# A third gate projection ahead of the last SSD output projection, memory norms inside the SSD, and a convolution that goes on below later projections

## The chip, the cores and the metric

The kernel runs on one core of a Trainium2 chip. The metric is device time in microseconds (us) of one execution. Five engines work in parallel, each through its own rows in order: TensorE (PE in the profile, with its weight loads as PEld), VectorE (DVE), ScalarE (ACT), GpSimd (POOL) and SyncE (SP, which here only starts DMAs; ACT and POOL start some too). An engine waits for another by semaphores.

## What is computed

One layer of a streaming encoder with 512 prompt tokens, 64 sample tokens and 256 memory rows. The normed input goes through one large projection, three branches are computed from it and merged by sigmoid gates:

```python
h = _rmsnorm(x, norm_pre_w); proj = h @ w_in     # split: glu_v, glu_g, conv_gate, z, xbc, dt, q, xa_gate, gates
u = glu_v * jax.nn.sigmoid(glu_g)
c, new_a = _causal_dwconv(u, st_a, conv_dw_w, conv_dw_b)         # width 31
c = jax.nn.silu(_layernorm(c, conv_ln_w, conv_ln_b)) * jax.nn.silu(conv_gate)
out_a = c @ conv_out_w
y, new_h = _ssd_scan(xh, dt, a, B, C, st_h)                      # 4 groups of 8 heads
yg = (y + xh * ssd_d) * silu(z)                                  # per group:
yg = yg * lax.rsqrt(jnp.mean(yg * yg, axis=-1, keepdims=True) + EPS)
out_b = (yg * ssd_norm_w) @ ssd_out_w
k, v = split(_rmsnorm(mem, mem_norm_w) @ xa_kv_w)                # prompt memory; the sample uses a cache
p = jax.nn.softmax(einsum(q, k) * 256 ** -0.5); o = einsum(p, v)  # 4 heads
out_c = (o * jax.nn.silu(xa_gate)) @ xa_out_w
m = g[0] * out_a + g[1] * out_b + g[2] * out_c                   # g = sigmoid(gates + gate_b)
x_new = x + _rmsnorm(m @ w_out, norm_post_w)
```

All data are float32. Matmuls run on operands that are split into a high and a low part, with three products (high·high, high·low, low·high), so a projection of 128 output channels over 576 tokens and 1024 inputs is 2 × 8 × 3 = 48 matmuls.

## The kernel before

Channels lie on partitions and the T = 576 tokens along the free axis. The program is one stream of stages; in the profiled execution they lie as follows.

- **SSD, 0 to 440 us**: four groups of heads. For group g, `gating_a` (from L627) makes the sum of squares, `gating_b` (from L644) the norm: two ones-matmuls (L649, L650) sum over partitions, ACT takes the root (L652), DVE the reciprocal (L653) and the product (L657), and a high/low split follows (L616, L618). `out_b` then projects the group; its four weight tiles are named ob0_0 to ob3_3. The output projections of groups 0 to 2 are fill work of the next group's scan.
- **End of the SSD, 440 to 500 us**: `glu(0)`, `gating_b(3)`, `glu(1)`, the combinations T1 to T4 of the input for the next stage, `out_b(3, ...)`, `glu(2)`. A `glu(j)` is two projections, gg (its tanh on ACT) and gv (the product on DVE), and puts the result into the convolution's buffer `u`; POOL copies its tails (L736 to L740).
- **Pairs, 500 to 720 us**: 17 pairs of projections in a scheme of seven products P1 to P7 (`slot`, L905). DVE and ACT form the sums of weights (L875 to L888) and combine the products. Gated results go out through rows of the buffer `ob` to DRAM (msc, L944). At product P5 of pair 8, `mem_prep` loads the 256 memory rows into rows of `ob` that a store has freed (L1004) and norms them: Square and Sqrt on ACT (L270, L271), reciprocal and product on DVE (L272, L274).
- **Start of attention, 720 to 740 us**: q0, q1, then eight transposes of the memory to channels on partitions (`tr_act`, PE L331, ACT L333, DVE L334).
- **Attention, 740 to 890 us**: for each head, k and q of two tiles each, then the transposes of the head before (P, L1174), its output, then v, scores (L1113 to L1115) and softmax (L1098 to L1107). q0 and q1 come from the stage before; heads 1 to 3 project q between the k projections. cg0 and cg1 follow.
- **Merges, 890 to 1100 us**: `oc` (8 projections of the attention output), `cg2` to `cg7` (conv gates), `g0` (8 first merge gates), `oa` (8 projections of the convolution branch). `ln_mean` and `ln_rstd` do the layer norm over channels with ones-matmuls (L1265, L1266); between them and `oa`, channel tile by channel tile, stand the product with the norm, a tanh, the product with the gate and a split (L1300 to L1308, L620).
- **w_out and the last norm, 1100 to 1141 us.**

**The convolution** is background work: 8 channel tiles, each with a first step on ACT, 30 taps on DVE (L816, 606 columns, of which 576 count) and an `add` that sums over channels into `csum`. These steps lie in a list `bg`; `bgrun(n)` emits the next n at a place of the program, at raised priority. Places with a `bgrun`: every other product in the pair stage, the projections, scores and outputs of attention (2 to 6 each time), the oc merges (10 each); `bgrun(10000)` behind them emits the rest.

**The order on each engine** is made by a scheduler that simulates the program's dependencies; a priority moves an instruction forward. What an engine does first is therefore seen in its rows, not in the code.

**Weights**: the list `order` names each weight tile in the order of use; two tiles ahead (LA), `prep_to` loads one by SP into one of three buffers, makes the high part on ACT (L189) and the low part in one of two ways: a subtraction on DVE (L191), used up to the position `hold` (all that comes before attention) and for k and v, or a negated copy on ACT (L193) to which a DMA of POOL adds the raw weights (L194).

## Time and profile before

| what | us |
|---|---|
| median of 3 executions (1141.1 to 1145.8) | 1141.92 |
| the profiled execution itself | 1143.13 |
| its span in the profile | 1141.4 |
| mean granted clock of PE | 0.986 |

A window of the profile is read as: window, its length, then busy time and number of instructions for PE, PEld, DVE, ACT and POOL, the clock that PE was granted, the busy share of the DMA engines, GB/s. The stages of the program:

```profile
0.00:440.00 440.00, 435.46 (x3351) 415.54 (x3352) 344.73 (x598) 233.76 (x449) 41.84 (x122) 1.00 0.41 115
440.00:500.00 60.00, 47.00 (x340) 45.03 (x339) 45.70 (x63) 24.23 (x34) 13.23 (x12) 0.89 0.20 58
500.00:720.00 220.00, 211.44 (x1559) 208.83 (x1558) 165.51 (x246) 142.26 (x247) 60.30 (x65) 0.99 0.80 189
740.00:890.00 150.00, 142.11 (x1050) 135.88 (x1048) 139.65 (x214) 87.72 (x168) 9.49 (x11) 0.97 0.64 162
1100.00:1141.40 41.40, 34.48 (x152) 23.86 (x150) 17.31 (x33) 11.89 (x28) 0.00 (x0) 0.98 0.17 58
```

A busy PE is not PE at its peak: a matmul that runs at a lower clock is busy for longer. A line of the timeline gives start, duration, engine, line and operation, output and inputs, shapes, and in brackets how long the engine was idle before it and who released it.

### The profile page before, as it was taken

To read this page: it belongs to the slowest core of one execution; us is meant where nothing else is said; L and a number is where in the kernel's file an instruction comes from. 1 tells how busy PE (TensorE), PEld (TensorE's weight loads), DVE (VectorE), ACT (ScalarE), POOL (GpSimd) and SP (SyncE) were. 2 spreads that over 40 slices of the span, in tenths; PEclk is the share of its full clock that TensorE was granted. 3 is DMA by queue.
4 is the path that set the end of the run, shared out by engine and by line. 5 is a ranking of instruction groups with operands and counts; after the bars stand their busy time and mean duration, and the time that the engine had idled before them with its cause. 6 is when DMAs were issued, how large, how long until landed. Compare 5 with 4: busy or idle time off the path is not lost.

```text
span 1141.4 us, 20485 instructions
## 1 busy us (share of the span) xinstructions
PE 1097.9 (96%) x8081; PEld 1052.2 (92%) x8081; DVE 868.8 (76%) x1371; ACT 606.4 (53%) x1065; POOL 148.3 (13%) x237
## 2 busy tenths in 40 slices
PE   8999999999999999599989999899999999999997
PEld 8999999999999999599989999899898999999974
DVE  5778898488969886946787887389999998685433
ACT  5665655464537432535676666474457234685331
POOL 0100110020002100313224321000001011111000
PEclk9999999999999999799999999999999999999999
DMA  7354423442443323167887887666567786788812
GB/s 204 94 169 130 126 83 107 123 113 79 116 115 99 93 63 100 37 144 153 209 198 158 182 211 198 180 161 167 147 161 185 206 208 150 160 180 196 230 45 83
DMA packets 201495, 164.55 MB, mean 144 GB/s; under 512 B 14935, under 2 KB 175743, under 8 KB 201399
## 3 DMA queue, kind: packets, MB, share of 16 engines
q1 hardware_dynamic: 187142, 126.55, 38.8%
q0 software_dynamic: 13104, 34.35, 16.7%
...
## 4 chain that ended last, share of the span: by engine, by line
PE 84%; DVE 7%; issue 3%; DMA 3%; ACT 2%; POOL 0%; DVEq 0%; SPq 0%; ACTq 0%; POOLq 0%
PE mm L214 55%; PE X L905 7%; DVE c L816 3%; PE Y L905 3%; PE ps L214 3%; PE Z L905 2%; PE ps L1114 2%; PE ps L1115 2%; PE ps L1113 2%; DMA pl<-rawb 2%; PE ps L573 2%; PE ps L599 2%; PE ps L577 1%; DVE wlo L191 1%; PE ps L538 1%
## 5 line engine op out<-in xcount | busy, mean ns | idle before, releaser
L214 PE MATMUL mm<-hT,whi 128*128 128x288 f32 (+2 forms) x2240 | 397.3, 297 | 1.0 <-ACT ob L668 0.5
L214 PEld LDWEIGHTS mm<-hT,whi 128*128 128x128 f32 x2240 | 334.3, 189 | 3.4 <-issue 1.3
L214 PE MATMUL mm<-hT,wlo 128*128 128x288 f32 (+2 forms) x1120 | 246.4, 298 | 0.0
L189 ACT ACTIVATE whi<-raw 128x1024 fp32r<-128x1024 f32 x118 | 124.8, 1057 | 216.2 <-PE mm L214 169.1
L816 DVE SCALAR_TENSOR_TENSOR c<-u,dww,c 128x606 f32<-128x606 f32 x240 | 199.6, 846 | 2.8 <-ACT c L809 0.3
L214 PEld LDWEIGHTS mm<-hT,wlo 128*128 128x128 f32 x1120 | 184.8, 189 | 1.3 <-issue 0.7
L191 DVE TENSOR_TENSOR wlo<-raw,whi 128x1024 fp32r<-128x1024 f32 x78 | 95.2, 1221 | 51.2 <-ACT whi L189 50.8
L214 PE MATMUL mm<-hi,whi 128*128 128x288 f32 x512 | 112.3, 301 | 10.8 <-DVE xs L657 10.8
L214 PE MATMUL mm<-lo,whi 128*128 128x288 f32 x512 | 111.4, 298 | 3.8 <-DVE lo L618 3.8
L214 PE MATMUL mm<-hi,wlo 128*128 128x288 f32 x512 | 110.9, 297 | 0.0
L214 PEld LDWEIGHTS mm<-hi,whi 128*128 128x128 f32 x512 | 83.3, 191 | 12.2 <-ACT hi L616 11.0
L214 PEld LDWEIGHTS mm<-lo,whi 128*128 128x128 f32 x512 | 83.3, 190 | 4.4 <-DVE lo L618 4.4
L214 PEld LDWEIGHTS mm<-hi,wlo 128*128 128x128 f32 x512 | 83.2, 189 | 0.2 <-issue 0.2
L194 POOL DMA_DIRECT2D wlo<-raw x40 | 34.7, 868 | 329.9 <-ACT wlo L193 257.4
L466 DVE SCALAR_TENSOR_TENSOR acc<-xp,scw,acc 128x579 f32<-128x579 f32 x72 | 58.3, 815 | 3.1 <-ACT acc L462 1.9
L193 ACT ACTIVATE wlo<-raw 128x1024 fp32r<-128x1024 f32 x40 | 42.0, 1049 | 27.8 <-PE ps L214 27.8
L888 DVE TENSOR_TENSOR wlo<-sm,whi 128x1024 fp32r<-128x1024 f32 x34 | 41.5, 1222 | 12.1 <-ACT whi L887 11.9
L875 ACT ACTIVATE ph<-rawb 128x512 fp32r<-128x512 f32 x34 | 21.4, 631 | 49.9 <-PE X L905 37.5
L877 POOL DMA_DIRECT2D pl<-rawb x34 | 29.9, 887 | 96.7 <-ACT pl L876 71.3
L458 POOL COPY tails<-xp 128x3 f32<-128x3 f32 x24 | 17.3, 720 | 193.3 <-ACT xp L456 187.8
L887 ACT ACTIVATE whi<-sm 128x1024 fp32r<-128x1024 f32 x34 | 35.8, 1055 | 11.4 <-PE X L905 7.5
L559 ACT ACTIVATE M<-R,tok 128x128 f32<-128x128 f32 (+1 forms) x80 | 24.8, 380 | 12.3 <-PE ps L599 12.3
...
## 6 DMA issues: line engine op xcount, KB each, us to landing
raw<-in_w_in_dram SPq DMA_DIRECT2D x70, 512.0 KB
wlo<-raw POOLq DMA_DIRECT2D x40, 512.0 KB, 5.7
...
R<-scr SPq DMA_DIRECT2D x16, 512.0 KB
raw<-in_ssd_out_w_dram SPq DMA_DIRECT2D x16, 512.0 KB
raw<-in_xa_kv_w_dram SPq DMA_DIRECT2D x16, 512.0 KB
```

The costliest lines, as they stand in the source:

```text
L189: a = nc.scalar.activation(hi[:, :n_], raw[:, :n_], AF.Copy)
L191: b = nc.vector.tensor_tensor(lo[:, :n_], raw[:, :n_], hi[:, :n_].bitcast(F32), ALU.subtract)
L193: nc.scalar.activation(lo[:, :n_], raw[:, :n_], AF.Copy, scale=-1.0)
L194: nc.gpsimd.dma_start(out=lo[:, :n_], in_=raw[:, :n_], accum_op=ALU.add)
L214: m = nc.tensor.matmul(o, lhsT=w, rhs=r[:, s:s + w_], start=(i == 0 and a == 0), stop=(i == n - 1 and a == 2),)
L466: nc.vector.scalar_tensor_tensor(acc, xp[:, r:r + 579], w4[:, r, jt:jt + 1], acc, ALU.mult, ALU.add)
L559: nc.scalar.activation(M[:, 4 + e, :], R[:nl, 4 + e, :], AF.Relu, scale=-1.0, bias=tok[:nl, 0, c, a + 4:a + 5])
L816: nc.vector.scalar_tensor_tensor(c, upad[j][:, r:r + NC], w31[:, r, j:j + 1], c, ALU.mult, ALU.add)
L877: nc.gpsimd.dma_start(out=lo, in_=src, accum_op=ALU.add)
L887: nc.scalar.activation(hi, sm, AF.Copy)
L888: nc.vector.tensor_tensor(lo, sm, hi.bitcast(F32), ALU.subtract)
L905: nc.tensor.matmul(o, lhsT=w[:, k], rhs=r[:, k], start=(start and k == 0 and a == 0), stop=(k == 3 and a == 2), skip_group_check=True,)
```

## The change

- Gate 2 of the GLU (gg2, gv2) is projected with gates 0 and 1, ahead of `out_b(3, ...)`. In its old place q2 and q3 are projected, copied by ACT and spilled to DRAM by a DMA of ACT's queue; head 1 loads them back through SP instead of projecting them.
- The low parts of the weights from gg0 on (six of gates, four of ob3) are made by ACT and POOL's DMA, no longer by DVE.
- The sums of squares of the memory rows, their roots and reciprocals are made in the SSD, beside the root of `gating_b(0)` and `gating_b(1)`, from a load of their own (L649 of the changed kernel). In the pair stage stay the load into `ob` (at P5 of pair 7) and a product on DVE (L1030, at P5 of pair 9).
- Background steps: two of three products up to product 60 and then every other one in the pair stage; 2, 3 or 4 where attention had 3, 4 or 6; 5 at each merge in place of 10. Behind the merges the list `late` (cg2 to cg6, g0_0 to g0_3, cg7, g0_4 to g0_7) sets the order: seven steps behind each of its first five projections, then the rest; `ln_mean` behind g0_0, `ln_rstd` behind g0_3; g0_4 to g0_7 stand at every second step of the loop that applies the norm.
- The convolution's result is compacted from 606 to 576 columns as soon as it is whole (two ACT copies in place of one); sums, layer norm and the product with the gate run on 576 columns, that product as one instruction in place of two.
- At the start of attention four of the memory's transposes stand ahead of q0 and four ahead of q1, and the first weights of attention are prepared behind the last P6.

```diff
-    csum = crp.tile([128, NC], F32, name="csum")
+    csum = crp.tile([128, T], F32, name="csum")
...
-    spill = {k: dram.tile([8, 128, T], F32, name=f"spill_{k}") for k in ("xg", "g2")}
+    spill = {k: dram.tile([8, 128, T], F32, name=f"spill_{k}") for k in ("xg", "g2", "q")}
...
-    for j in range(2):
+    for j in range(3):
         glu_jobs(j)
     for q in range(4):
         ob_job(3, q)
-    glu_jobs(2)
+    for i in (2, 3):
+        wjob(f"q{i}", w_in, C_Q + 128 * i)
     hold = len(order)
...
             wjob(f"k{i}", xa_kv_w, 128 * i)
-            if h > 0:
+            if h > 1:
                 wjob(f"q{i}", w_in, C_Q + 128 * i)
...
         wjob(f"oc{j}", xa_out_w, 128 * j)
-    for j in range(2, 8):
-        wjob(f"cg{j}", w_in, C_CG + 128 * j)
-    for j in range(8):
-        wjob(f"g0_{j}", w_in, C_G + 128 * j)
+    late = [("cg", j) for j in range(2, 7)] + [("g0_", j) for j in range(4)] + [("cg", 7)] + [("g0_", j) for j in range(4, 8)]
+    for k, j in late:
+        wjob(f"{k}{j}", w_in, (C_CG if k == "cg" else C_G) + 128 * j)
     for j in range(8):
         wjob(f"oa{j}", conv_out_w, 128 * j)
...
-                if nprep[0] < hold or name[0] in "kv":
+                if nprep[0] < pos["gg0"] or name[0] in "kv":
                     b = nc.vector.tensor_tensor(lo[:, :n_], raw[:, :n_], hi[:, :n_].bitcast(F32), ALU.subtract)
...
+    ssm = const.tile([128, 2, 4], F32, name="ssm")
+    mst = {}
+
+    def mem_stat_load(t):
+        mst[t] = sc.tile([128, D], F32, tag="M", name="mst")
+        nc.sync.dma_start(out=mst[t], in_=mem_prompt[0, 128 * t:128 * t + 128])
+
+    def mem_stat(t):
+        nc.scalar.activation(mst[t], mst[t], AF.Square, accum_out=ssm[:, t, 0:1])
+        nc.scalar.activation(ssm[:, t, 1:2], ssm[:, t, 0:1], AF.Sqrt, scale=1.0 / D, bias=eps1)
+        nc.vector.reciprocal(ssm[:, t, 2:3], ssm[:, t, 1:2])
...
+        if g < 2:
+            mem_stat(g)
         nc.vector.reciprocal(rs, rs)
...
         gating_a(g)
+        if g < 2:
+            mem_stat_load(g)
         if g < 3:
...
     gating_b(3)
     glu(1, s2, "acc", 2)
+    glu(2, s2, "acc", 2)
...
         out_b(3, q)
     st.close()
-    glu(2, sx, "bc", 4)
+    for i in (2, 3):
+        pt = proj(f"q{i}")
+        t = sx.tile([128, 640], F32, tag="bc", name="bc", bufs=4)[:, 0:T]
+        nc.scalar.activation(v2(t), va(pt), AF.Copy)
+        nc.scalar.dma_start(out=spill["q"][i], in_=t)
...
         def add():
+            cact[j] = upad[j][:, 0:T]
+            nc.scalar.activation(upad[j][:, 0:512], box[0][:, 0:512], AF.Copy)
+            nc.scalar.activation(upad[j][:, 512:T], box[0][:, 542:606], AF.Copy)
             if j == 0:
-                nc.vector.tensor_copy(csum, box[0])
+                nc.vector.tensor_copy(csum, cact[j])
             else:
-                nc.vector.tensor_tensor(csum, csum, box[0], ALU.add)
-            cact[j] = upad[j][:, 0:NC]
-            nc.scalar.activation(cact[j], box[0], AF.Copy)
+                nc.vector.tensor_tensor(csum, csum, cact[j], ALU.add)
...
 
+    def mem_load():
+        for t, (m_t, _) in enumerate(mt_):
+            nc.sync.dma_start(out=m_t, in_=mem_prompt[0, 128 * t:128 * t + 128])
+
     def mem_prep():
         for t, (m_t, _) in enumerate(mt_):
-            nc.sync.dma_start(out=m_t, in_=mem_prompt[0, 128 * t:128 * t + 128])
-            rms_tile(m_t, 128, obf[:, 2 * D:3 * D], ssx[:, t], None)
+            nc.vector.tensor_scalar(m_t, m_t, ssm[:, t, 2:3], None, ALU.mult)
 
     for i, (p, pr) in enumerate(seq):
-        if (p, pr) == (8, "P5"):
+        if (p, pr) == (7, "P5"):
+            mem_load()
+        if (p, pr) == (9, "P5"):
             mem_prep()
         while todo and todo[0][0] <= i:
             todo.pop(0)[1]()
         slot(p, pr)
-        if i % 2:
+        if (p, pr) == (np_ - 1, "P6"):
+            limit[0] = len(order)
+            prep_to(hold + LA - 1)
+        if i % (3 if i < 60 else 2):
             bgrun(1)
     stp.close()
     stp = ExitStack()
     pp_[0] = stp.enter_context(tc.tile_pool(name="pmm2", bufs=2, space=PSUM, reuse_waits="tile"))
     pp_[1] = stp.enter_context(tc.tile_pool(name="pps2", bufs=4, space=PSUM, reuse_waits="tile"))
     st.close()
-    limit[0] = len(order)
-    prep_to(hold + LA - 1)
+    stt.close()
     st = ExitStack()
     keep = st.enter_context(tc.tile_pool(name="keep", bufs=2, reuse_waits="tile"))
     st3 = ExitStack()
     a2 = st3.enter_context(tc.tile_pool(name="a2", bufs=2, reuse_waits="tile"))
     memp = st3.enter_context(tc.tile_pool(name="memp", bufs=1, reuse_waits="tile"))
-    stt.close()
     memT = [memp.tile([128, KD, NMEM], F32R, name=f"memT{i}") for i in range(2)]
-    q0 = [proj(f"q{i}") for i in range(2)]
-    for j in range(8):
-        tr_act(mt_, j, memT, V_MEM, NMEM)
+    q0 = []
+    for i in range(2):
+        for j in range(4 * i, 4 * i + 4):
+            tr_act(mt_, j, memT, V_MEM, NMEM)
+        q0.append(proj(f"q{i}"))
 
 
     for s, dst in ((0, o_csp), (1, o_css)):
...
             kfs.append(kv_proj(f"k{2 * h + i}", i, khi, klo))
-            pt = q0[i] if h == 0 else proj(f"q{2 * h + i}")
-            nc.scalar.activation(v2(qhi[:, i]), va(pt), AF.Copy)
-            nc.vector.tensor_tensor(v2(qlo[:, i]), va(pt), v2(qhi[:, i].bitcast(F32)), ALU.subtract)
-            bgrun(6)
+            if h == 1:
+                src = sx.tile([128, 640], F32, tag="bc", name="bc", bufs=4)[:, 0:T]
+                nc.sync.dma_start(out=src, in_=spill["q"][2 + i])
+                src = v2(src)
+            else:
+                src = va(q0[i] if h == 0 else proj(f"q{2 * h + i}"))
+            nc.scalar.activation(v2(qhi[:, i]), src, AF.Copy)
+            nc.vector.tensor_tensor(v2(qlo[:, i]), src, v2(qhi[:, i].bitcast(F32)), ALU.subtract)
+            bgrun(3)
...
-        bgrun(10)
+        bgrun(5)
...
         merge(j, 2, None, f"oc{j}", ocact)
+    sgs = dict(enumerate(sgl))
+    chl, g0t = [], []
+
+    def late_job(k, j):
+        if k == "cg":
+            sgs[j] = silu2(proj(f"cg{j}"), hlA, "hi", 8)
+        else:
+            g0t.append(gate_t(f"g0_{j}", 0, j, hlA, "lo", 8))
+
+    for e in late[:5]:
+        late_job(*e)
+        bgrun(7)
     bgrun(10000)
+    late_job(*late[5])
     ln_mean()
-    sgs = []
-    for j in range(8):
-        sgs.append(sgl[j] if j < 2 else silu2(proj(f"cg{j}"), hlA, "hi", 8))
-        if j == 4:
-            ln_rstd()
+    for e in late[6:9]:
+        late_job(*e)
+    ln_rstd()
+    late_job(*late[9])
 
     hl[0] = hlB
...
+        nc.vector.tensor_tensor(sg, sg, c, ALU.mult)
         chl.append(split(sg, 0.25))
-        g0t.append(gate_t(f"g0_{j}", 0, j, hlA, "lo", 8))
+        if j % 2:
+            late_job(*late[10 + j // 2])
     stx.close()
```

(`bgrun` numbers in attention, and HN → HA, NC → T in the layer norm, change likewise.)

**PE at the end of the SSD.** Before: the last rows of gv1's projection (inputs hT, weights whi and wlo), the ones-matmuls of `gating_b(3)` (th, tl), and ob3 (inputs hi and lo).

```order
L214 MATMUL mm<-hT_92,wlo 128x256
L214 MATMUL mm<-hT_92,wlo 128x320
L649 MATMUL ps<-th,onesr 128x288 x2
L650 MATMUL ps<-tl,onesr 128x288 x2
L214 MATMUL mm<-hi,whi 128x288 x4
L214 MATMUL mm<-lo,whi 128x288 x2
L214 MATMUL mm<-hi,wlo 128x288 x2
```

Now, around the same ones-matmuls (L661, L662), which stand inside gv1:

```order
L214 MATMUL mm<-hT_92,wlo 128x256
L661 MATMUL ps<-th,onesr 128x288 x2
L214 MATMUL mm<-hT_92,wlo 128x320
L214 MATMUL mm<-hT_92,whi 128x256
L214 MATMUL mm<-hT_92,whi 128x320
L214 MATMUL mm<-hT_93,whi 128x256
L214 MATMUL mm<-hT_93,whi 128x320
L662 MATMUL ps<-tl,onesr 128x288 x2
L214 MATMUL mm<-hT_92,wlo 128x256
```

Behind the last of these stand the other 25 rows of gv1 and the 96 of gg2 and gv2, and then the first of ob3: 122 matmuls lie between the ones-matmuls and ob3, where none did.

**DVE at the memory norms, in the pair stage.** Before (ct and ob: results of the products; c: a tap; sm, wlo: sums of weights and their low part; ssx: the norm's factor):

```order
L943 SCALAR_TENSOR_TENSOR ob<-ct,ob 128x576
L816 SCALAR_TENSOR_TENSOR c<-u,dww,c 128x606
L272 RECIPROCAL ssx<-ssx 128x1
L274 TENSOR_SCALAR ob<-ob,ssx 128x1024
L888 TENSOR_TENSOR wlo<-sm,whi 128x1024
L816 SCALAR_TENSOR_TENSOR c<-u,dww,c 128x606
L272 RECIPROCAL ssx<-ssx 128x1
L884 TENSOR_TENSOR sm<-raw,rawb 128x512
L274 TENSOR_SCALAR ob<-ob,ssx 128x1024
L888 TENSOR_TENSOR wlo<-sm,whi 128x1024
```

Now, at the first of the two:

```order
L965 SCALAR_TENSOR_TENSOR ob<-ct,ob 128x576
L837 SCALAR_TENSOR_TENSOR c<-u,dww,c 128x606 x2
L910 TENSOR_TENSOR wlo<-sm,whi 128x1024
L994 TENSOR_TENSOR ct<-u_6418,Y 128x288
L906 TENSOR_TENSOR sm<-raw 128x512
L906 TENSOR_TENSOR sm<-sm,rawb 128x512
L991 SCALAR_TENSOR_TENSOR ct<-X,ys 128x288
L980 TENSOR_TENSOR ct<-X,zs 128x288
L837 SCALAR_TENSOR_TENSOR c<-u,dww,c 128x606 x2
L1030 TENSOR_SCALAR ob<-ob,ssm 128x1024
L965 SCALAR_TENSOR_TENSOR ob<-ct,ob 128x576
L910 TENSOR_TENSOR wlo<-sm,whi 128x1024
```

The product with the norm has moved forward by more than a pair, to right behind the store and the load of its rows; the first row here is the last write to the rows that the load replaces.

**PE in attention, ahead of the transposes of head 0's P.** Before, they follow k2, q2, k3 and q3 (q: inputs hT):

```order
L214 MATMUL mm<-hT_92,whi 128x288 x2
L214 MATMUL mm<-hT_93,whi 128x288 x2
L214 MATMUL mm<-hT_92,wlo 128x288 x2
L1174 MATMUL ps<-ident,P 128x128 x8
L1181 MATMUL ps<-ident,P 128x64 x2
```

Now they follow k2 and k3 alone (inputs memT), 48 rows behind the last score:

```order
L1145 MATMUL ps<-cth,qlo 64x256
L214 MATMUL ps<-memT_8511,whi 128x256
L214 MATMUL ps<-memT_8512,whi 128x256
L214 MATMUL ps<-memT_8511,wlo 128x256
L214 MATMUL ps<-memT_8511,whi 128x256
```

```order
L214 MATMUL ps<-memT_8511,whi 128x256
L214 MATMUL ps<-memT_8512,whi 128x256
L214 MATMUL ps<-memT_8511,wlo 128x256
L1209 MATMUL ps<-ident,P 128x128 x8
L1216 MATMUL ps<-ident,P 128x64 x2
```

The 96 matmuls of q2 and q3 have left this place. The rows of k2 and k3 themselves and what follows the transposes are unchanged.

More of the change, by code (lines that the diff above doesn't have):

```diff
@@ L744, in glu @@
         pg = proj(f"gg{j}", HB)
-        t = pool.tile([128, 640 if tag == "bc" else T], F32, tag=tag, name=tag, bufs=bufs)[:, 0:T]
+        t = pool.tile([128, T], F32, tag=tag, name=tag, bufs=bufs)
         nc.scalar.activation(v2(t[:, 0:512]), pg[:, :, 0:256], AF.Tanh, scale=0.5)
@@ L1066, in v_proj @@
             )
-            bgrun(3)
+            bgrun(2)
         return pv
@@ L1077, in kv_proj @@
         nc.vector.tensor_tensor(klo[:, i], kf, khi[:, i].bitcast(F32), ALU.subtract)
-        bgrun(3)
+        bgrun(2)
         return kf
@@ L1157, in att_scores @@
             Ps.append(softmax(ps, n, cnt))
-            bgrun(3)
+            bgrun(2)
         return vhl, Ps
@@ L1200, in att_out @@
             nc.vector.scalar_tensor_tensor(oc[:, j, 512:T], po[:, 0:64], 0.5, sg[:, 512:T], ALU.mult, ALU.mult)
-            bgrun(4)
+            bgrun(3)
     last, sgl = None, []
@@ L1209, in hybrid_trunk_kernel @@
                 sgl.append(silu2(proj(f"cg{j}"), keep, "sg", 2))
-                bgrun(6)
+                bgrun(4)
         if last is not None:
@@ L1250, in merge @@
         pt = proj(oname, act=act)
-        bgrun(10)
+        bgrun(5)
         nc.vector.scalar_tensor_tensor(v2(t), v2(t), 1.0, va(pt), ALU.add, ALU.mult)
         nc.vector.tensor_tensor(ob[:, j], ob[:, j], t, ALU.add)
-    HN = [(0, 304), (304, 302)]
-    mean = e2.tile([128, NC], F32, tag="npw", name="mean", bufs=1)
+    mean = e2.tile([128, NC], F32, tag="npw", name="mean", bufs=1)[:, 0:T]
     def ln_sum():
-        sh = e2.tile([128, NC], F32R, tag="lsq", name="sh")
-        sl = e2.tile([128, NC], F32R, tag="lsq", name="sl")
+        sh = e2.tile([128, NC], F32R, tag="lsq", name="sh")[:, 0:T]
+        sl = e2.tile([128, NC], F32R, tag="lsq", name="sl")[:, 0:T]
         nc.scalar.activation(sh, csum, AF.Copy)
         nc.vector.tensor_tensor(sl, csum, sh.bitcast(F32), ALU.subtract)
-        pts = [ps_tile() for _ in HN]
-        for pt, (s, n) in zip(pts, HN):
+        pts = [ps_tile() for _ in HA]
+        for pt, (s, n) in zip(pts, HA):
             nc.tensor.matmul(pt[:, :n], lhsT=onesr, rhs=sh[:, s:s + n], start=True, stop=False)
@@ L1269, in ln_mean @@
     def ln_mean():
-        for pt, (s, n) in zip(ln_sum(), HN):
+        for pt, (s, n) in zip(ln_sum(), HA):
             nc.scalar.activation(mean[:, s:s + n], pt[:, :n], AF.Copy, scale=1.0 / D)
@@ L1276, in ln_mean @@
             else:
-                sq = e2.tile([128, NC], F32, tag="lsq", name="lsq")
+                sq = e2.tile([128, NC], F32, tag="lsq", name="lsq")[:, 0:T]
                 nc.scalar.activation(sq, cact[j], AF.Square)
@@ L1281, in ln_rstd @@
     def ln_rstd():
-        for pt, (s, n) in zip(ln_sum(), HN):
+        for pt, (s, n) in zip(ln_sum(), HA):
             nc.scalar.activation(mean[:, s:s + n], pt[:, :n], AF.Sqrt, scale=1.0 / D, bias=eps1)
@@ L1300, in hybrid_trunk_kernel @@
         nc.vector.tensor_tensor(c, c, mean, ALU.mult)
-        th = e2.tile([128, NC], F32, tag="lsq", name="th")
+        th = e2.tile([128, NC], F32, tag="lsq", name="th")[:, 0:T]
         lw, lb = V_LNW + j, V_LNB + j
```

3 lines of the change are left out of this document (removed).

## The prediction

> **What bounds the kernel now.** The page's busy shares and its chain come first:
>
> ```profile
> PE 1097.9 (96%) x8081; PEld 1052.2 (92%) x8081; DVE 868.8 (76%) x1371; ACT 606.4 (53%) x1065; POOL 148.3 (13%) x237
> PE 84%; DVE 7%; issue 3%; DMA 3%; ACT 2%; POOL 0%; DVEq 0%; SPq 0%; ACTq 0%; POOLq 0%
> ```
>
> TensorE (PE) is the bound, 84% of the chain. The change adds or removes almost no matmuls, so it can gain only where PE waits or runs at a lower clock. The windows by stage say where that is (columns: window; us; busy us and count of PE, PEld, DVE, ACT, POOL; granted clock; DMA share; GB/s):
>
> ```profile
> 462.50:476.50 14.00, 2.23 (x11) 1.65 (x9) 14.00 (x18) 7.58 (x11) 3.59 (x2) 0.67 0.14 38
> 476.50:482.90 6.40, 5.21 (x29) 5.21 (x30) 6.40 (x10) 1.89 (x3) 5.20 (x2) 0.67 0.00 0
> 482.90:560.00 77.10, 77.06 (x580) 76.83 (x579) 50.79 (x72) 40.07 (x66) 19.94 (x26) 1.00 0.69 160
> 560.00:600.00 40.00, 35.02 (x244) 33.86 (x244) 31.02 (x47) 27.69 (x49) 8.58 (x10) 0.96 0.84 201
> 720.00:740.00 20.00, 17.56 (x122) 16.22 (x121) 7.90 (x13) 7.80 (x15) 0.00 (x0) 0.92 0.72 202
> 890.00:1100.00 210.00, 209.79 (x1520) 206.84 (x1521) 147.97 (x207) 98.78 (x126) 23.48 (x27) 1.00 0.76 183
> ```
>
> Where PE is full (482.9 to 560) a matmul takes 77.10/580 = 0.133 us, so a projection of 48 takes 6.4. By that price the windows lose: 462.5 to 482.9, 20.4 − 40 × 0.133 = **15.1 us**; 560 to 600, 40 − 32.5 = **7.5**; 720 to 740, 20 − 16.2 = **3.8**; the merges, 890 to 1100, nothing. The list of PE's waits names the owners:
>
> ```profile
> PE mm L214 <- DVE xs L657: 10.8, 1, 10.8
> PE mm L214 <- DVE lo L618: 3.8, 2, 2.2
> PE Y L905 <- ACT whi L887: 3.5, 2, 2.1
> PE ps L331 <- DVE memT L334: 2.3, 1, 2.3
> ```
>
> **A: the third gate ahead of the last SSD projection.** The timeline of the norm's chain (start, duration, engine, instruction):
>
> ```profile
> 462.98 0.43 PE L650 MATMUL ps<-tl,onesr 128*128 128x288 f32 x2
> 463.72 1.28 ACT L652 ACT_TABLE_LOAD   x1
> 467.02 3.75 DVE L653 RECIPROCAL rs<-rs 128x576 f32<-128x576 f32 x1
> 472.63 3.00 DVE L657 SCALAR_TENSOR_TENSOR xs<-xs,vecs,rs 128x576 f32<-128x576 f32 x4
> 474.21 1.33 PE L214 MATMUL mm<-hi,whi 128*128 128x288 f32 x4 [10.81 <-DVE xs L657]
> 479.56 0.75 DVE L618 TENSOR_TENSOR lo<-xs,hi 128x576 fp32r<-128x576 f32 x1
> 477.76 6.00 POOL L737 COPY u<-sta 128x30 f32<-128x30 f32 x1
> ```
>
> Before, nothing stands between the ones-matmuls (end 463.4) and the first ob3 matmul (474.2). After, 26 matmuls of gv1 and 96 of gate 2 do: 122 × 0.133 = 16.2 us. The first operand is needed after 10.8 us and the last lo (480.3, 16.9 after) three quarters into ob3_0, at 16.2 + 2.4 = 18.6. All is covered, with 1.7 us to spare at the end. The 96 matmuls of q2, q3 take gate 2's old place; the 12.8 us that they cost are paid back in attention (D). Ten lo parts (six of gates, four of ob3) leave DVE (1221 ns each in the page's groups) for ACT and a POOL DMA, which the page's list of issues lands after 5.7 us:
>
> ```profile
> L191 DVE TENSOR_TENSOR wlo<-raw,whi 128x1024 fp32r<-128x1024 f32 x78 | 95.2, 1221 | 51.2 <-ACT whi L189 50.8
> ...
> wlo<-raw POOLq DMA_DIRECT2D x40, 512.0 KB, 5.7
> ```
>
> They queue on POOL behind the copies of convolution tails (6.00 us in the timeline above), so ob3_1 and ob3_2 are the weights that may come late, by up to 6 us together. DVE is full in both windows (14.00 of 14.00, 6.40 of 6.40), so the 12.2 us help its other work there. I take **−14**, between −9 and −15.1. The idle also lowered the clock (0.67 in both windows); that goes with it. The Trainium skill, page "TensorE: Matmul & The Clock Gate" (Part 1: The HAM clock gate), says that an idle window of about 3.4 us halves the clock until about 3.4 us of work have passed; by it the 10.8 and 2.2 us of waiting would cost some 1.7 us more, 14.7 in all, and the trace's 15.1 agrees.
>
> The memory rows' sums of squares now stand in gating 0 and 1 (two Squares, two Sqrts beside a Sqrt that is there anyway). ACT is busy 53% of the span and has room beside PE there, so 0; if it had none, their 2 × 1.06 us (the Squares of B) would show: 0 to +2.
>
> **B: the pair stage loses the memory norms.** On ACT, beside the worst stretch of the stage:
>
> ```profile
> 580.00 1.06 ACT L270 ACTIVATE ob<-ob 128x1024 f32<-128x1024 f32 x1 [1.59 <-issue]
> 583.17 1.28 ACT L271 ACT_TABLE_LOAD   x1
> 589.83 1.28 ACT L941 ACT_TABLE_LOAD   x1
> ```
>
> Two Squares and two table loads, 4.7 us, leave ACT, ahead of the weight copies (L887) for which PE waits 3.5 us in two waits; with their share of the clock (0.96 of 40 us is 1.6 lost) I take **−4** of the 7.5. The Trainium skill, page "ScalarE: Activation LUTs" (What ACT_TABLE_LOAD costs), puts a table load at about 2.7 us; here it took 1.28, and by the page B would be 2.8 larger. Against it: on DVE the scaling of the memory rows now stands right behind the loads, and each load behind the store that frees its rows:
>
> ```profile
> 549.28 0.34 SPq L944 DMA_DIRECT2D msc<-ob  x1
> 553.80 0.34 SPq L1004 DMA_DIRECT2D ob<-in_mem_prompt_dram  x1
> 585.31 7.92 SPq L944 DMA_DIRECT2D msc<-ob  x2
> ```
>
> A store frees its rows 4.5 us after its issue (549.28 to 553.80) and a load takes about as long, so the scaling can run some 10 us after the row that was stored; the DVE rows between sum to 7 and 9 us. So DVE stalls 2 to 4 us twice, and what queues behind (weight sums, T operands) is a pair ahead of PE: 84 matmuls, 11.2 us. I cost it at 0; without that cover it is up to +6. Bounds of B: −7.5 and +3.
>
> **C: the start of attention.** The transposes of memory stand between the q0 and q1 projections, four and four, not in a row of eight; the weights are prepared one product earlier. The 2.3 us wait for DVE's memT goes: **−2.5** of 3.8, bounds −3.8 and 0.
>
> **D: attention.** By heads (from one head's transposes of P to the next's):
>
> ```profile
> 739.40:777.65 38.25, 37.41 (x297) 36.68 (x296) 31.67 (x47) 25.05 (x49) 1.73 (x2) 0.99 0.58 148
> 777.65:813.72 36.07, 34.29 (x261) 32.83 (x260) 35.61 (x56) 19.89 (x39) 1.72 (x2) 1.00 0.62 163
> 813.72:850.32 36.60, 35.29 (x259) 34.02 (x259) 34.04 (x53) 18.59 (x36) 1.88 (x3) 0.95 0.60 159
> 850.32:880.66 30.34, 27.81 (x206) 26.41 (x207) 28.99 (x48) 18.83 (x37) 4.17 (x5) 0.99 0.73 171
> 880.66:890.00 9.34, 7.91 (x31) 6.54 (x31) 9.34 (x16) 5.37 (x10) 0.00 (x0) 0.66 0.78 194
> ```
>
> In the first stretch PE sets the time, in the others DVE (35.61 of 36.07). The code asks for far fewer taps here, but the scheduler fills them in again: its order has 100 in attention, before 111. That is 11 × 0.846 = 9.3 us of DVE, and two channel sums (0.7 each) go to the pair stage; counted row by row, 5.5 of it falls into the first stretch, 5 into the others.
>
> ```profile
> L816 DVE SCALAR_TENSOR_TENSOR c<-u,dww,c 128x606 f32<-128x606 f32 x240 | 199.6, 846 | 2.8 <-ACT c L809 0.3
> ...
> 755.41 0.28 PE L1115 MATMUL ps<-cth,qlo 128*64 128x256 f32 x1
> 765.69 0.49 ACT L1107 ACTIVATE P<-P,mx 64x256 f32<-64x256 f32 x1
> 774.06 1.04 PE L1174 MATMUL ps<-ident,P 128*128 128x128 f32 x8
> ```
>
> The first stretch gives up 12.8 us of PE. But from the last score (755.7) to the last softmax row (766.2) pass 10.5 us, and then 18.4 us of k2, q2, k3, q3 covered them; now k2 and k3 alone do, 48 matmuls of 256 columns, 48 × 0.133 × 256/288 = 5.7. **A new wait of 4.8 us**, and what the clock loses by it: 880.66 to 890 lost 9.34 × 0.34 = 3.2 around several waits; for one I take half, 1.6. So −12.8 + 4.8 + 1.6 = −6.4 there and −5 in the DVE-bound stretches: −11.4 against the −12.8 that pay A's move, D = **+1** (−5 to +6: the softmax quicker on a freer DVE, or no gain in the later heads).
>
> **E: convolution later, layer norm below the late gates.** 76 taps are left for the merges (72), and the merges' PE is full, so only lateness counts. The first layer-norm sum moves from behind cg7 to behind g0_2: DVE's rows up to it sum to 85 us, PE reaches it 104 us after the first oc matmul; no wait. The second leaves less:
>
> ```profile
> 1003.95 3.94 DVE L1284 RECIPROCAL mean<-mean 128x606 f32<-128x606 f32 x1 [5.67 <-ACT mean L1283]
> 1034.82 1.43 DVE L620 SCALAR_TENSOR_TENSOR lo<-hi 128x576 fp32r<-128x576 f32 x2 [0.59 <-ACT hi L616]
> ```
>
> Reciprocal to last lo part took 32.3 us, some 35 from the ones-matmuls, with 221 matmuls (29.4 us) between these and oa0; with oa0 and oa1 themselves that was enough, PE did not wait. Now 129 (17.2 us) are left. At 576 columns the chain is some 33; oa0 and oa1 would be done at 17.2 + 12.8 = 30.0, but their last 8 matmuls start at 33: +4.1, with some clock **+5** (0 to +12, if DVE arrives late).
>
> **Sum**: −14 −4 −2.5 +1 +5 = −14.5. The profiled execution took 1143.13 us (span 1141.4), 1.2 over the median of 1141.92: 1128.6 on its scale, **1127** on the median's.
>
> **Rivals.** (1) *The new waits are hidden*: DVE is less loaded, softmax and layer norm finish sooner, D −5 and E 0: 1142 − 25.5 = 1116. For it: DVE's 12 us less at the end of SSD. Against: both chains run ACT and DVE in turn, and load hardly enters. (2) *A wait takes the place of the one removed*: POOL's late lo parts hold ob3 (A −9), head 1 gives nothing to the later heads (D +4), layer norm runs late (E +8): −3.5 with B and C, 1138, 1135 to 1143. For it: POOL's copies above, DVE's lateness in attention. Against: POOL is busy 13% of the span. (3) *Slower*: the memory loads. SP issues in order, and the row at 585.31 shows it held 7.9 us by a store; if a store and its load are each held so, both times, DVE stands 18 to 20 us at each scaling row. Of each, a pair's lead covers 11.2; the rest, 14 to 18 us in sum, is PE's, and up to 3 more by the clock (a third of 9 us). Only above 14.5 us is the kernel slower than before: 1142 to 1149. Against: the loads stand at the same place in SP's queue as before, where they were issued without such a wait. (4) *The change doesn't do what it says*: ob3 still waits for its norm; the order excludes it.
> By the clock rule of the Trainium skill (the page and section named under A) waits under 3.4 us would cost no clock, so E would be 1 us less and head 1, above it, about as I took it. The trace speaks against the first: 0.66 in 880.66 to 890, with PE idle 1.4 us.
>
> **How the numbers follow.** Forecast 0.6 (1118 to 1136), rival 1 0.18, rival 2 0.17, rival 3 0.04, rival 4 0.01. The range reaches to most of rivals 1 and 2: 1111 to 1140. Faster by over 0.5% (about what a measurement of this kernel can tell from no change) means below 1136.2: the forecast nearly whole, rival 1 and a little of rival 2, 0.84; same 0.12; slower 0.04.
>
> **What would show it.** A right: no PE wait above 2 us and clock 1.00 between the ones-matmuls and the end of ob3; wrong: waits of ob3 for wlo. B: no table load of L271, no wait of Y for whi above 1 us; wrong: DVE idle over 8 us at the memory scaling. C: 720 to 740's wait for memT gone. D: a PE wait of 4 to 5 us at head 0's transposes of P, attention about 11 us shorter. E: PE waits of 3 to 5 us in oa0 and oa1. The forecast fails most easily if D's wait and E's wait are both misjudged the same way, as both rest on latencies taken from a fuller DVE.

## The result, and the profile after

The changed kernel took **1127.66 us** (median of 1123.87, 1125.52, 1129.81, 1130.06), the kernel before, run beside it, 1141.87: a ratio of 0.9866 with a 95% interval of 0.9826 to 0.9906, so 14 us or 1.3% faster. The profiled execution is the quickest of the four, 1123.87 (span 1122.2, mean clock 0.996 where before had 0.986). The busy shares of its page:

```profile
PE 1090.6 (97%) x8081; PEld 1045.0 (93%) x8081; DVE 853.3 (76%) x1353; ACT 619.5 (55%) x1087; POOL 154.1 (14%) x247
```

As many matmuls as before, in 7.3 us less of busy time: what went is waiting, and the low clock around it. The windows of the changed kernel (columns as before) at the places of the prediction's terms:

```profile
0.00:440.00 440.00, 433.13 (x3336) 413.26 (x3337) 341.56 (x597) 243.61 (x462) 50.07 (x125) 1.00 0.43 119
...
462.50:482.90 20.40, 20.40 (x155) 20.40 (x154) 18.91 (x25) 14.39 (x20) 10.17 (x15) 1.00 0.61 132
...
560.00:600.00 40.00, 39.29 (x295) 38.84 (x295) 37.80 (x57) 26.98 (x49) 10.75 (x14) 1.00 0.93 222
...
722.00:732.00 10.00, 10.00 (x82) 9.98 (x81) 5.35 (x8) 4.51 (x9) 0.00 (x0) 1.00 0.34 104
```

Where the last norm of the SSD left PE 40 matmuls in 20.4 us, there are now 155, at full clock; 560 to 600 holds 295 instead of 244; the start of attention is full. The first row speaks against the change: 440 us of SSD hold 15 matmuls fewer than before (3351). The list of PE's waits:

```profile
PE ps L1209 <- ACT P L1137: 4.1, 2, 2.2
...
PE mm L214 <- DMA wlo<-raw: 1.8, 1, 1.8
...
PE Z L927 <- DMA pl<-rawb: 1.4, 2, 0.8
...
PE mm L214 <- DVE lo L618: 0.9, 1, 0.9
...
PE ps L573 <- ACT bt L535: 0.8, 2, 0.5
...
PE mm L214 <- DVE lo L620: 0.4, 2, 0.3
PE Y L927 <- ACT whi L909: 0.4, 1, 0.4
```

The 10.8 us for `xs` are gone, as is the wait for memT, and Y's wait for whi fell from 3.5 to 0.4. New are 4.1 us for head 0's P and 1.8 us for a weight's low part in `oa`. The timeline of the changed kernel's PE shows both:

```profile
477.75 0.43 PE L214 MATMUL mm<-hT,wlo 128*128 128x256 f32 x2
478.02 0.42 PE L214 MATMUL mm<-hi,whi 128*128 128x288 f32 x2
...
744.24 0.28 PE L1145 MATMUL ps<-cth,qlo 128*64 128x256 f32 x1
...
752.43 1.12 PE L1209 MATMUL ps<-ident,P 128*128 128x128 f32 x4 [2.16 <-ACT P L1137]
755.45 1.12 PE L1209 MATMUL ps<-ident,P 128*128 128x128 f32 x4 [1.90 <-ACT P L1137]
...
1010.11 0.42 PE L214 MATMUL mm<-lo,whi 128*128 128x288 f32 x2
1012.35 0.54 PE L214 MATMUL mm<-hi,wlo 128*128 128x288 f32 x2 [1.81 <-DMA wlo<-raw]
```

ob3 (478.02) follows gate 2 without a gap; the transposes of P wait twice, 8 us behind the last score (744.24).

For the stages, the same matmul of each kernel is taken as a mark in the trace: the last state matmul of the SSD's scan (L573), the first and the last product of the pair stage, the first k projection, the first `oc`, the last `oa`. "Again" is a second profile of the changed kernel (below); its execution took 1128.41.

| stage (us) | before | changed | again |
|---|---|---|---|
| start to last state matmul | 441.5 | 442.4 | 445.2 |
| to first pair product | 75.8 | 74.0 | 74.0 |
| pair stage | 202.8 | 197.2 | 198.5 |
| to first k projection | 18.9 | 14.8 | 14.8 |
| attention, to first oc | 148.7 | 136.0 | 136.4 |
| merges, to last oa | 194.9 | 198.9 | 199.0 |

The second row holds q2 and q3, 12.8 us, in the changed kernel alone. Term by term against the prediction (q2 and q3 counted in D, as there):

| term | predicted | changed | again |
|---|---|---|---|
| memory statistics in the SSD | 0 | +0.9 | +3.6 |
| A, gate 2 ahead of ob3 | −14 | −14.6 | −14.6 |
| B, pair stage | −4 | −5.6 | −4.3 |
| C, start of attention | −2.5 | −4.1 | −4.1 |
| D, attention | +1 | +0.1 | +0.5 |
| E, merges | +5 | +4.0 | +4.1 |
| sum | −14.5 | −19.3 | −14.8 |

"Again" stands near the median, so its column is the one to hold against the time. The row of the memory statistics is all that the SSD's length changed by, whatever its cause.

### The profile page after: what moved, and what is told of

Same layout as the page of the kernel before. It is cut to its first block, busy times and chain, and to the rows that moved or that the text cites. A ratio compares the mean times of both kernels' runs of the same rounds, so it can differ in the third digit from the quotient of the medians.

```text
span 1122.2 us, 20502 instructions
## 1 busy us (share of the span) xinstructions
PE 1090.6 (97%) x8081; PEld 1045.0 (93%) x8081; DVE 853.3 (76%) x1353; ACT 619.5 (55%) x1087; POOL 154.1 (14%) x247
## 4 chain that ended last, share of the span: by engine, by line
PE 86%; DMA 4%; issue 3%; ACT 3%; DVE 2%; SPq 0%; POOL 0%; DVEq 0%; ACTq 0%; POOLq 0%
PE mm L214 54%; PE X L927 8%; PE ps L214 4%; PE Y L927 4%; PE ps L1144 2%; PE ps L1143 2%; PE ps L1145 2%; PE Z L927 2%; PE ps L573 2%; PE ps L599 1%; PE ps L577 1%; DMA pl<-rawb 1%; DMA mst<-in_mem_prompt_dram 1%; DMA ob<-in_x_prompt_dram 1%; DMA raw<-in_w_in_dram 1%
## 5 line engine op out<-in xcount | busy, mean ns | idle before, releaser
L191 DVE TENSOR_TENSOR wlo<-raw,whi 128x1024 fp32r<-128x1024 f32 x68 | 83.0, 1220 | 36.8 <-ACT whi L189 35.6
L194 POOL DMA_DIRECT2D wlo<-raw x50 | 43.9, 878 | 405.6 <-ACT wlo L193 356.2
L193 ACT ACTIVATE wlo<-raw 128x1024 fp32r<-128x1024 f32 x50 | 52.4, 1048 | 26.1 <-PE ps L214 25.1
```

The lines of the kernel that those rows point to most:

```text
L191: b = nc.vector.tensor_tensor(lo[:, :n_], raw[:, :n_], hi[:, :n_].bitcast(F32), ALU.subtract)
L193: nc.scalar.activation(lo[:, :n_], raw[:, :n_], AF.Copy, scale=-1.0)
L194: nc.gpsimd.dma_start(out=lo[:, :n_], in_=raw[:, :n_], accum_op=ALU.add)
```

## The experiments

All are edits of the changed kernel (a line with − is the changed kernel's; the cuts leave out lines of the same kind), and each computes the whole layer. Ratios are to the kernel before, run beside it on the same chip, with their 95% intervals.

### The changed kernel again

> The changed kernel once more, unaltered. Four executions lay between 1123.9 and 1130.1 us, a spread of 6 where the kernel before mostly stays within 1. Theory: one or two waits for transfers (the weights' low parts that POOL adds by DMA) land late in some executions; then a profile above 1127 shows a wait for wlo of 2 us or more that the profile at 1123.9 does not have, at ob3 or oa. Rival: the whole program runs a little slower (lower granted clock everywhere); then no single wait grows.

Measured: 1127.6 us, 0.9868 (0.9849 to 0.9886). The spread of some 5 us between executions is not the late weight of `oa` (that wait was 1.6 us, against 1.8). Between the two profiles it lies in the SSD (2.7 us) and the pair stage (1.3). In the SSD one piece can be seen; windows of "again", and then of the changed kernel's first profile:

```profile
104.00:128.00 24.00, 23.05 (x175) 21.34 (x173) 15.73 (x32) 14.90 (x28) 2.01 (x6) 1.00 0.47 149
128.00:153.00 25.00, 25.00 (x186) 24.42 (x186) 23.75 (x41) 17.96 (x35) 10.67 (x14) 0.93 0.36 107
```

```profile
104.00:128.00 24.00, 23.50 (x177) 21.32 (x175) 16.04 (x30) 15.70 (x30) 2.26 (x7) 1.00 0.48 143
128.00:153.00 25.00, 25.00 (x201) 24.76 (x201) 24.42 (x44) 19.04 (x33) 11.68 (x16) 1.00 0.42 121
```

A wait for `bt` of 1.0 us instead of 0.5 comes just ahead of a stretch at a clock of 0.93 in place of 1.00: 25 × 0.07 = 1.7 us lost behind half a microsecond more of waiting. The 0.93 is an average: from 129.2 to 132.5 the clock stood at 0.50, beside that at 1.00. What makes `bt` late is the subject of "Memory norms back" and "Statistics tied".

### A undone: gate 2 back behind ob3, q2 and q3 back in head 1

```diff
-    glu(2, s2, "acc", 2)              # ahead of out_b(3, ...)
...
-    for i in (2, 3):
-        pt = proj(f"q{i}")
...
+    glu(2, sx, "bc", 4)
```

> Gate 2 back behind ob3 and q2, q3 back in head 1; all else as in the change. Theory (the fill between the ones-matmuls and ob3 is what gained 15 us): the wait of ob3 for the norm returns, 10 us or more, 15 us with its clock; head 1's waits (4.1 us, some 1.5 of clock) go. 1127.7 + 15 - 5.5 = 1137, and head 0 to head 1 is again 35 us. Rival (DVE's 12.2 us of lo parts that moved to ACT and POOL are what freed the norm's chain): the wait for the norm stays under 4 us and the time is 1122 to 1128.

Measured: 1147.41 us, 1.0045 (1.0025 to 1.0064). Without A the rest of the change is slower than the kernel before. Its PE waits:

```profile
PE mm L213 <- ACT hi L615: 6.8, 1, 6.8
PE mm L213 <- DMA wlo<-raw: 4.6, 2, 2.4
PE mm L213 <- DVE lo L617: 4.1, 2, 2.7
```

The expectation was 1137. The ten low parts are off DVE here too, and 10.6 us still pass from the ones-matmuls to ob3 (before 11.1): what A brings is the fill, not DVE's relief. By the marks, against the first profile of the changed kernel, 13.9 us come back at the SSD's end, as A had it; the rest is 6.4 in the pair stage (203.6, where PE waits 2.4 us for gate 2's product `u`), 1.5 in attention and 2.8 in the merges.

### Only q2 and q3 back

```diff
-    for i in (2, 3):
-        pt = proj(f"q{i}")                 # behind ob3, spilled
...
+            src = va(q0[i] if h == 0 else proj(f"q{2 * h + i}"))
```

> Gate 2 stays ahead of ob3, but q2 and q3 are projected in head 1 again, nothing is spilled, and the pair stage follows ob3 directly. Theory: the 96 matmuls of q cover head 0's softmax and its two waits (4.1 us) go with their clock, A stays whole: 1127.7 - 5 = 1122 to 1124. Rival: the place behind ob3 was needed to cover the start of the pair stage (T operands and the first sums of weights on DVE and ACT); then PE waits 5 to 8 us there and the time is 1127 to 1131.

Measured: 1131.57 us, 0.9911 (0.9896 to 0.9926). Head 1's wait for P is gone, and nothing is won: attention takes 148.6 us, which without the 12.8 of q2 and q3 is 135.8, as before and after the change. The loss is in the pair stage, 203.7 against 197.2, whose operands now come late:

```profile
PE Z L920 <- DMA pl<-rawb: 4.2, 5, 1.1
...
PE Y L920 <- ACT whi L902: 1.5, 2, 1.2
```

So q2 and q3 behind ob3 also give the pair stage's loads and sums a start ahead of PE. The prediction saw in that place only a price.

### Only q3 back

```diff
-    for i in (2, 3):
+    for i in (2,):
         pt = proj(f"q{i}")
```

> Only q3 goes back into head 1; q2 stays behind ob3. 48 matmuls (6.4 us) cover each place. Theory: head 0's softmax needs 11.7 us from the last score to its last row and would have 5.7 + 6.4 = 12.1: its waits fall from 4.1 to under 1 us, and the pair stage's start has 6.4 us of cover: 1122 to 1124, the best of the three. Rival: the waits of head 1 come from ACT's and DVE's order (they work on the k projections ahead of the softmax) and move along: no change, 1126 to 1129.

Measured: 1124.47 us, 0.9847 (0.9831 to 0.9864), 3 us below the changed kernel, though the interval overlaps that of "again" (0.9849 to 0.9886). One projection behind ob3 is enough for the pair stage (196.3), and one in head 1 covers the softmax: no wait for P is left. Attention without q3's 6.4 us is 135.8 again, so D's wait as such cost nothing net.

### Ten low parts on DVE again

```diff
-                if nprep[0] < pos["gg0"] or name[0] in "kv":
+                if nprep[0] < hold or name[0] in "kv":
```

> The ten lo parts of gates 0 to 2 and ob3 are made by DVE again; all else as in the change. Theory: DVE has to do 12.2 us more between gate 0 and the end of ob3, where it is busy 18.9 of 20.4 us, so the norm's chain ends later than its cover of 16.2 us: a wait of 3 to 8 us of ob3 for the norm, 1130 to 1136. Rival (the fill alone matters, the chain comes first on DVE by priority): no wait over 1 us, 1126 to 1129; if POOL's late lo parts cost something there, even 1124.

Measured: 1129.67 us, 0.9904 (0.9888 to 0.9920): 2 us slower by the medians, 4 by the ratios. ob3 waits 0.3 us for the norm, where 3 to 8 were expected. From the last state matmul to the end of ob3 pass 61.8 us, against 61.1 in the changed kernel, and from there to the pair stage nothing changes; attention has 1.8 us more than in "again", with 3.4 us more at a clock of 0.50 (from 862.3). With the fill in place, DVE's 12.2 us are worth some 2 to 4, and at ob3 itself 0.7.

### Memory norms back in the pair stage

```diff
-        if g < 2:
-            mem_stat(g)
...
-            nc.vector.tensor_scalar(m_t, m_t, ssm[:, t, 2:3], None, ALU.mult)
+            nc.sync.dma_start(out=m_t, in_=mem_prompt[0, 128 * t:128 * t + 128])
+            rms_tile(m_t, 128, obf[:, 2 * D:3 * D], ssx[:, t], None)
...
-        if (p, pr) == (9, "P5"):
+        if (p, pr) == (8, "P5"):
```

> The memory norms as before: load, Square, Sqrt, reciprocal and product at P5 of pair 8; nothing in the SSD. Theory: the pair stage gets its 5.6 us back, with PE waits for weight copies of ACT near the Squares and two more table loads: 1127.7 + 5 = 1133. Rival: the pair stage got shorter by other parts (T operands earlier, other places of the taps): no change, 1126 to 1129.

Measured: 1127.47 us, 0.9880 (0.9862 to 0.9899): the same as the changed kernel. The pair stage takes 201.8, as B said (+4.6 and +3.3 against the two profiles). But the scan's last state matmul stands at 440.5, not at 442.4 or 445.2. **B's gain is real, and the SSD gives back a part of it that varies.** In the nine profiles of this study with the statistics inside the scan that matmul stands at 442.1 to 445.2 us, 443.7 in the mean; in the five others at 440.5 to 443.7, 441.6 in the mean. The equal medians say that about all of B's gain is lost; the marks place some 2 us of it. The changed kernel's timeline of ACT at the end of group 0's scan, where before had no table load at all, shows how:

```profile
116.82 1.06 ACT L652 ACTIVATE mst<-mst 128x1024 f32<-128x1024 f32 x1 [2.40 <-DMA mst<-in_mem_prompt_dram]
...
119.53 1.28 ACT L653 ACT_TABLE_LOAD   x1
120.83 0.29 ACT L653 ACTIVATE ssm<-ssm,eps 128x1 f32<-128x1 f32 x1
...
122.31 1.28 ACT L562 ACT_TABLE_LOAD   x1
...
125.90 0.26 ACT L535 ACTIVATE bt<-ps 64x128 f32<-64x128 f32 x1
```

The statistics are written beside the root of `gating_b`, but nothing ties them to it. They depend on their load alone, so the scheduler's order put them some 30 us ahead of it: the root of `gating_b(0)` comes at 151.7, the Square at 116.8, among the last steps of group 0's scan and the first exponentials of group 1's. The second set stands at 221 to 228, its root at 256.5. ACT waits 2.4 us for the rows, then loads the table of the root and, 2.8 us later, that of the scan's exponentials again. `bt`, which PE needs for the last state matmul of group 0, stands behind all of it (125.90, in this run 120.10).

The rows hold up DVE too. Their tile has the tag "M", so it takes one of the two buffers of the scan's M, and DVE starts the next M only behind the Square. The row in the changed kernel, and the same one in this run:

```profile
118.00 0.87 DVE L556 TENSOR_SCALAR M<-R,tok 128x128 f32<-128x128 f32 x4 [2.60 <-ACT mst L652]
```

```profile
112.94 0.87 DVE L556 TENSOR_SCALAR M<-R,tok 128x128 f32<-128x128 f32 x4
```

### Statistics tied to gating's root

```diff
-    def mem_stat(t):
-        nc.scalar.activation(mst[t], mst[t], AF.Square, accum_out=ssm[:, t, 0:1])
+    def mem_stat(t, rs):
+        nc.vector.tensor_scalar(ssm[:, t, 3:4], rs[:, 0:1], 0.0, None, ALU.mult)
+        nc.scalar.activation(mst[t], mst[t], AF.Square, bias=ssm[:, t, 3:4], accum_out=ssm[:, t, 0:1])
```

The bias is zero times gating's root, so that the Square cannot be placed ahead of it.

> The changed kernel with the memory statistics held behind gating's root: the bias of the Square is a zero that DVE makes from the root's output, so Square and Sqrt cannot run before it. On ACT the order then has 15 table loads, as the kernel before; the change has 17. Theory (in the change the scheduler pulled both into the next group's scan, where ACT stood 2.4 to 2.7 us for the load of the rows and loaded two more tables each time, so that PE waited and in some executions lost its full clock): the 2 to 4 us of the SSD go, its marks fall on those of the kernel before, 1123 to 1125, all executions within 3 us. Rival: the SSD's cost is the rows' load and ACT's Square wherever they stand: 1126 to 1129, spread as before.

Measured: 1127.45 us, 0.9880 (0.9863 to 0.9897). PE does not wait for `bt` at that place, and the last state matmul stands at 441.5. M stands even later than in the changed kernel (132.87), so its buffer alone is not what held PE. The expectation puts the statistics into the next group's scan; they stood ahead of their root, which is what the tie forbids. It takes away one pair of table loads, that of group 1; group 0's Sqrt now comes late and still has its own (157.62 and 160.56).

The time did not follow: against the first profile attention grew by 1.0 us and the merges by 1.2, and the executions spread as before (1125.7 to 1130.3). In the two kernels below that keep the tie, the last state matmul stands at 443.7 and 440.7; in the first of them PE waits 1.2 us at 437 for a load of the scan's state, as in two other profiles of this study (1.1 and 1.6).

Of the profiles of this study, the nine with the statistics inside the scan show a wait for `bt` of 0.4 to 1.0 us between 104 and 140 us, the five others none; two of the nine, those with 0.9 and 1.0, show a clock of 0.72 from 128 to 134, all others 1.00. So this and the load of the state are sources of the spread, and not the whole of it.

### Background numbers back

```diff
-        if i % (3 if i < 60 else 2):
+        if i % 2:
...
-            bgrun(3)
+            bgrun(6)
...
-        bgrun(5)
+        bgrun(10)
```

> The numbers of background steps as before (every other product in the pair stage; 3, 4 and 6 in attention; 10 at each oc merge); the order of the late projections stays. In the order on DVE 57 taps stand ahead of attention, 91 in it and 92 behind it (the change: 64, 102, 74). Theory: attention, bound by DVE in its later heads, gets shorter by some of the 11 taps (up to 9 us of DVE), and the first layer-norm sum, reached by PE 20 us after DVE has its operand, comes late by nothing: 1120 to 1126. Rival: 18 more taps (15 us) behind attention make the layer norm late, PE waits there: 1129 to 1136.

Measured: 1129.65 us, 0.9899 (0.9883 to 0.9915), as the rival had it. Attention took 135.7, with 91 taps on DVE in place of 100; so the taps do not set its length. The merges took 205.4, with the layer norm late in `oa`:

```profile
PE mm L214 <- ACT hi L616: 4.6, 1, 4.6
```

### Order of the late projections back

```diff
-    late = [("cg", j) for j in range(2, 7)] + [("g0_", j) for j in range(4)] + [("cg", 7)] + [("g0_", j) for j in range(4, 8)]
+    late = [("cg", j) for j in range(2, 8)] + [("g0_", j) for j in range(8)]
...
```

> The order of the late projections as before: all conv gates, then all first merge gates with the layer norm's application between them; background steps are emitted behind oc; numbers of background steps as in the change. Theory: the merges' 4 us come from the layer norm's end standing too close to oa0; with eight merge gates below it they go: 1123 to 1125. Rival: the merges' loss is a late lo part of oa0's weights from POOL's DMA and stays: 1126 to 1129.

Measured: 1127.75 us, 0.9887 (0.9867 to 0.9908): no difference. The scheduler again puts some 130 matmuls (129) between the second layer-norm sum and `oa`; that number follows from when the channel sum is whole, that is from the background's pace, not from the list.

### Low parts of oa0 and oa1 on DVE

```diff
-                if nprep[0] < pos["gg0"] or name[0] in "kv":
+                if nprep[0] < pos["gg0"] or name[0] in "kv" or name in ("oa0", "oa1"):
```

> The changed kernel with the low parts of oa0 and oa1 made by DVE. PE's one long wait in the merges, 1.6 to 2.2 us for a low part from POOL's DMA at oa1, then has no cause. Theory (layer norm's chain on DVE stands right behind it): DVE, full there (4.4 of 4.4 us), is 2.4 us later, the wait goes over to the operands' low or high parts: 1127 to 1129. Rival (only the DMA is late): 1124 to 1126.

Measured: 1129.64 us, 0.9897 (0.9880 to 0.9914), 2 us slower. The wait for the weight goes and comes back as one for the norm's chain, which stood right behind it:

```profile
PE mm L214 <- DVE lo L620: 2.4, 3, 0.8
```

### Tied, and 177 matmuls between the layer norm and oa

"Statistics tied", and more of the convolution in the oc merges, so that the channel sum is whole earlier:

```diff
-        bgrun(5)
+        bgrun(12)
```

> As stat_tied, and 12 background steps at each oc merge in place of 5. In PE's order 177 matmuls then stand between the second layer-norm sum and oa0, where the change and stat_tied have 130. Theory (the merges' 4 us come from the layer norm's end standing too close to oa0 and oa1): PE's waits there go, 3 to 5 us below stat_tied: 1119 to 1122. Rival (what PE waits for there is POOL's low part of oa1, late by its own DMA): same as stat_tied within 1.

Measured: 1124.16 us, 0.9852 (0.9839 to 0.9866), 3.3 us under "Statistics tied". 177 matmuls now lie between the second sum and `oa`, where 130 did; the waits for the weight and the norm in `oa` are gone but for 0.3 us, and the merges take 195.9 instead of 200.1. E's reason is shown by this and by the other kernels: with some 130 matmuls there the merges take 198.6 to 201.7 us in ten profiles, with 72 ("Background numbers back") 205.4, with 177 195.9 here and 194.3 in the last kernel.

### What works, together

q3 in head 1, the statistics tied, and `bgrun(10)` at each merge.

> q3 back in head 1, the memory statistics held behind gating's root, and 10 background steps at each oc merge (177 matmuls between the second layer-norm sum and oa0). If the three gains are of different places they add: 3 (q3_back) + 3 (SSD) + 4 (merges) below 1127.6: 1117 to 1120, below every kernel so far. Rival: attention's length is set by DVE, so q3's place gains nothing of its own: 1120 to 1123.

Measured: **1119.26 us**, 0.9815 (0.9802 to 0.9828): faster than both kernels, 8 us under the changed one. It is 4.9 us under "Tied, and 177 matmuls", from which it differs in q3's place and in 10 steps for 12. By the marks, 3.0 of these fall into the SSD, 1.6 into the merges and 1.3 into attention, and the start of the pair stage loses 1.0; how much is owed to q3's place is not shown by that. The longest of its PE waits:

```profile
PE Z L928 <- DMA pl<-rawb: 2.0, 2, 1.1
PE ps L1145 <- DVE ptl L1214: 2.0, 2, 1.4
PE ps L1144 <- ACT pth L1213: 1.7, 1, 1.7
```

## Why the prediction came out right

The forecast was 1127 us, the median is 1127.66, and the likeliest case, the balance of the six terms, is what happened. Rival 1 (new waits hidden) fell: both waits are in the trace. Rival 2 (a wait in place of the one removed) fell at ob3, which waits for no weight. Rival 4 fell with the order. One step was wrong, and another step's reason. That the median lies within 1 us of the forecast is luck in part: in "again", +3.6 us that the prediction had at 0 stand against 3.9 us by which A to E together came out better than forecast.

**A** held: 122 matmuls in the gap, no PE wait between 455 and 520 us, clock 1.00; −14.6 against −14.

**The memory statistics at 0: the step that failed.** The prediction had "two Squares, two Sqrts beside a Sqrt that is there anyway" and took ACT's 53% as room. The Sqrts do not lie beside the other one. Each stands alone among a scan's exponentials, some 30 us ahead of that root, and brings a table load before and one after; ACT waits for the rows, and DVE for their buffer. Measured, +0.9 and +3.6 in the two profiles, the second beyond the bound of +2, and 2.1 between the means of the nine profiles with them in the scan and the five without. Only the rows of ACT in the changed order show this; a share of busy time cannot.

**B** had its size, −5.6 and −4.3 against −4, and its reason: no table load in the stretch, 0.4 us for whi. The stall that it set against that came once, in the second scaling on DVE:

```profile
557.33 0.75 DVE L1030 TENSOR_SCALAR ob<-ob,ssm 128x1024 f32<-128x1024 f32 x1
...
571.12 0.75 DVE L1030 TENSOR_SCALAR ob<-ob,ssm 128x1024 f32<-128x1024 f32 x1 [2.07 <-DMA ob<-in_mem_prompt_dram]
```

2.07 us, and PE waited for none of it; the lead of a pair covered it. With it falls rival 3, which needed 18 to 20 us at each.

**C** was under-sized: −4.1 against −2.5, a little beyond its bound of −3.8. All of the lost time went, not the named wait alone; the window 722 to 732 is full.

**D** had the right sum for a reason that is half right. The first stretch (k0 to head 0's P) fell by 11.0 us, and two waits, 2.16 and 1.90, came in place of the 4.8 counted; the second falls into the next stretch, which grew by 2.4. The windows around them:

```profile
744.20:750.30 6.10, 6.08 (x51) 5.88 (x49) 6.10 (x14) 4.14 (x10) 0.00 (x0) 1.00 0.81 229
750.30:752.40 2.10, 0.00 (x0) 0.00 (x0) 2.10 (x4) 2.10 (x6) 0.00 (x0) 1.00 0.20 65
752.40:753.50 1.10, 1.07 (x4) 0.61 (x4) 1.10 (x2) 1.10 (x5) 0.00 (x0) 0.53 0.92 274
753.50:756.50 3.00, 1.10 (x6) 0.61 (x5) 2.96 (x7) 1.90 (x7) 0.00 (x0) 0.50 0.63 158
756.50:760.00 3.50, 3.50 (x16) 2.83 (x16) 3.46 (x6) 2.34 (x5) 0.00 (x0) 0.60 0.34 102
```

The busy time at the low clock, 1.07 × 0.47 + 1.10 × 0.50 + 3.50 × 0.40, is 2.5 us, where 1.6 were taken; from 752.5 to 759.2 the clock stood at 0.50. The Trainium skill, page "TensorE: Matmul & The Clock Gate", section "Part 1: The HAM clock gate", lowers the clock after an idle window of about 3.4 us; here the row right behind a single wait of 2.16 us is at 0.53, so the trace does not agree with that length. "DVE sets the later heads" did not hold: with 91 or 100 taps, and with q2 and q3 in head 1 or out of it, attention less these two is 135.7 to 136.4 in the kernels that differ in these (137.5 with gate 2 back). Behind the second stretch attention lost 4.1 us, where the prediction had 5 for fewer taps. There the kernel before had its clock at 0.50 twice, from 815.3 to 818.7 and from 880.1 to 887.0, and the changed kernel never: 10.2 × 0.50 = 5.1 us, which would be enough for it. What holds the length otherwise is not settled; in the two longest (138.3 and 138.8) the clock stood at 0.50 for 10.2 us, in the changed kernel for 6.8.

**E** had its size, +4.0 against +5. Its first wait is not the norm but oa1's low part: `oa0` and `oa1` go channel by channel together, so oa1's weight is needed within the first matmuls. POOL's row in the timeline is this:

```profile
1004.05 0.86 POOL L194 DMA_DIRECT2D wlo<-raw  x1 [4.11 <-ACT wlo L193]
```

From its issue to the matmul that used it pass 8.3 us, where such a DMA took 5.7 in the median before (8.4 at most) and 5.2 in this kernel. The norm's chain stands right behind, as the low parts on DVE showed; more matmuls ahead cured both.

The 1.3 us between the two profiles in the pair stage are a late part of a weight and the clock behind it. In "again":

```profile
606.11 0.40 PE L927 MATMUL Z<-hT,pl 128*128 128x288 f32 x1 [1.41 <-DMA pl<-rawb]
```

```profile
607.10:610.30 3.20, 3.20 (x15) 3.20 (x14) 2.77 (x4) 0.00 (x0) 0.80 (x1) 0.50 0.92 250
```

The first profile waits for `pl` 0.8 us at most and shows no low clock in that stage. What stays open is why such loads land late in some executions, and why "Statistics tied" did not gain what its SSD did.
